# Value products of causal attention: the low part of the weights multiplies 128 columns of the values instead of 256

## The chip, the core and the metric

The kernel runs on one core of one Trainium2 chip. The metric is the device time of one execution in microseconds (us), the median of several runs. Lower is better.

## The reference

One decoder block on a sequence of 1024 tokens with 1024 channels, all in float32. One wide projection feeds two mixers, a causal pooling mixer and a causal differential attention with four heads; sigmoid gates merge them, an output projection and a gated feed-forward part follow. The part that matters here is the attention:

```
def block(args):                       # one block of 128 queries
    ...
    a = probs(qa, k1) - lam * probs(qb, k2)
    return jnp.einsum('bhqk,bhkd->bhqd', a.astype(vh.dtype), vh)
```

`probs` is a causal softmax with a linear position bias. The `einsum` at the end is the value product: for every head (4) and every block of 128 queries (8), the weights `a` of the keys up to the diagonal are multiplied with the values `vh`, 128 channels per head.

## The kernel before

Every float32 matrix product is made of products of two parts. An operand `x` is kept as a high part, which TensorE reads in its fast float32 form, and a low part, which is `x` minus the high part. A product of two matrices is then normally three matmuls: high by high, high by low and low by high (`triple`, L233 to L235). ScalarE (ACT) makes the high part by a copy, VectorE (DVE) the low part by a subtraction (`sub`, L89).

The kernel goes through these stages: the input projection with all its operands, the attention, the output projection with a norm, the gate and up projections of the feed-forward part, and the down projection. The large projections use a seven-product scheme (`seven`) in place of eight.

The attention works on 32 rows; a row is one head and one block of 128 queries, with up to eight blocks of 128 keys. For a row:

- `scores` (L750, L751) makes the scores of both softmaxes on TensorE; DVE adds the bias and finds the extremum (L754), ACT takes the exponential (L757), DVE combines both maps (L762, L763).
- `transposes` (L778) turns each 128x128 block of the map on TensorE into a bank of PSUM, ACT copies out the high part (L780) and DVE subtracts out the low part (L89); both go to a tile `AT`, index 0 the high part, index 1 the low part.
- `values` (L792) multiplies. The stationary operand is a 128x128 block of `AT`, high or low; the moving operand is `V[:, b, :, :]`, 256 columns: 128 of the values' high part and beside them 128 of their low part. The result has 256 columns, which ACT and DVE scale and add at the end (L797, L798). So both parts of the weights meet both parts of the values, four partial products in two matmuls per block.

A row with n key blocks has 2n such matmuls, 288 in all.

While the attention waits for DVE and ACT, TensorE is given filler: the rest of the last unit of the input projection, then the branch product of the pooling mixer (`branch(0, ...)`), then the branch product of the attention output (`branch(1, ...)`), which show as `branch` at L233 to L235. The order in which rows and filler are written comes from a loop with costs (`step`, `value_cost` and others); the change leaves these costs alone. The loop's code stands outside of the blocks with a manual schedule, so the order in which each engine gets its instructions is decided when the kernel is built, by the scheduler of the framework.

At the end of the attention, `head_norm` (DVE at L811) scales the last head, and `turn_head` transposes its output on TensorE (`oT`, L826) and splits it on ACT and DVE (`OTh`, `OTl`, L828, L829). The branch product of the attention reads the weights of `w_branch_b` (`load_w`: DMA at L96 into `wb_raw`, the high part `wb_hi` on ACT, the low part `wb_lo` by L89) and the stored gates (`sgs`, DMA at L689). Both DMAs are issued by one queue, SP's, in order. `wb_raw` has two buffers, so that a load waits until the subtraction for the load two before is done. With the gates DVE scales `ma` (L162) and later adds the branch product (`take_b`, L162). The banks of PSUM for `aT` and for the value product `o` come from one pool of two, tag `mm`.

Of the kernel before, what the change touches and what calls it, by code (L numbers as in the profile page):

```python
# [15 lines left out]
P = 128  # L16
# [25 lines left out]
def block_kernel(ctx, tc, x, w_in, pool_mix, pool_scale, w_branch_a, lam_q1, lam_k1, lam_q2,  # L42
                 lam_k2, subln_g, w_branch_b, w_out, mix_pre_g, mix_post_g, ffn_pre_g, ffn_post_g,
                 w_ffn_gate, w_ffn_up, w_ffn_down, out):
    nc = tc.nc
# [27 lines left out]
    def mm(s):  # L73
        return ps.tile([P, HALF], F32, tag="mm", bufs=2, name=name(s))

    def fil(s):
        return ps.tile([P, HALF], F32, tag="fil", bufs=2, name=name(s))
# [51 lines left out]
    def sumsq(src, ss):  # L129
        nc.scalar.activation(junk[:, :src.shape[-1]], src, AF.Square, accum_out=ss)  # L130
# [235 lines left out]
    o = [(fil("q"), fil("k")), (mm("q"), mm("k"))]  # L366
# [47 lines left out]
    with tc.manual_schedule(engines={nc.tensor.engine, nc.scalar.engine, nc.vector.engine, nc.gpsimd.engine}):  # L414
# [81 lines left out]
        o = fil("q"), fil("k")  # L496
# [6 lines left out]
        o = mm("q"), mm("k")  # L503
# [219 lines left out]
    def value_cost(n, last):  # L723
        return 0.24 * n, 0.35 if last else 0.0
# [61 lines left out]
    def values(h, qb):  # L786
        V = heads[h][3]
        ats, rec = attends[h, qb]
        o = mm("o")[:, :2 * P]
        for b in range(qb + 1):  # L790
            for j in range(2):
                nc.tensor.matmul(o, ats[b // 4][:, j, b % 4 * P:(b % 4 + 1) * P], V[:, b, :, :],  # L792
                                 start=b == 0 and j == 0, stop=b == qb and j == 1)
            if b == 3 and qb > 3:
                yield value_cost(4, False)
        ov = O[h][:, qb, :]
        nc.scalar.mul(ov, o[:, P:], rec[:, 0:1])  # L797
        nc.vector.scalar_tensor_tensor(out=ov, in0=o[:, :P], scalar=rec[:, 0:1], in1=ov,  # L798
                                       op0=ALU.mult, op1=ALU.add)
        sumsq(ov, oss[h][:, qb:qb + 1])  # L800
        yield value_cost(qb % 4 + 1 if qb > 3 else qb + 1, True)
# [87 lines left out]
    for i in range(-AHEAD, len(seq)):  # L889
        j = i + AHEAD  # L890
        if j < len(seq):
            h, pos = divmod(j, len(QORDER))
            if pos == 2 and 0 < h < NH - 1:
                for _ in load_head(h + 1):
                    pass
            step(scores(*seq[j]))
        j = i + 1
        if 0 <= j < len(seq):
            step(transposes(*seq[j]))
        if i >= 0:  # L900
            step(values(*seq[i]))
            h, pos = divmod(i, len(QORDER))
            if h < NH - 1 and pos == len(QORDER) - 1:
                head_norm(h)
            elif h == NH - 1 and pos < NH - 1:
                for t in range(2):
                    turn_head(pos, t)
            elif h == NH - 1 and pos % 4 == 3:
                b = slice(4, 8) if pos == 3 else slice(0, 4)
                head_norm(h, b)  # L910
                defer(LAG, partial(turn_head, h, b.start // 4))
# [138 lines left out]
    with tc.manual_schedule(engines={nc.tensor.engine, nc.scalar.engine, nc.vector.engine, nc.gpsimd.engine}):  # L1050
        o = [fil("wo") for _ in range(2)]
# [225 lines left out]
    for n, (i, kb) in enumerate(stream):  # L1277
        fetch(n + DEPTH + 3)
        if n + DEPTH < len(stream):
            j, kj = stream[n + DEPTH]  # L1280
# [5 lines left out]
        o = (Y, X, Y, X, Y, Z, Y)[i]  # L1286
# [46 lines left out]
```

## Time and profile before

| what | value |
|---|---|
| median of 3 runs | 1269.61 us |
| lowest and highest of the runs | 1268.1 and 1271.04 us |
| the profiled execution: span from its first to its last instruction | 1265.6 us |
| TensorE matmul (PE) busy | 1246.5 us, 98% |
| weight loads (PEld) busy | 1039.1 us, 82% |
| DVE, ACT, POOL busy | 838.6, 582.7, 142.7 us |
| mean granted TensorE clock | 0.998 |

For the profiled execution the span is the only time given; what lies around it (start and end of the program) is not in the trace, and the median of the timed runs is 4.0 us above the span. "PE" is TensorE's matmuls, "PEld" its weight loads, which overlap with matmuls; "SPq" is a DMA issue by SyncE's queue. Matmuls are pipelined: the recorded duration of one is longer than the distance to the start of the next, so that distance is what a matmul costs in a run of them.

### The profile page before, as it was taken

To read this page: it belongs to the slowest core of one execution; us is meant where nothing else is said; L and a number is where in the kernel's file an instruction comes from. 1 tells how busy PE (TensorE), PEld (TensorE's weight loads), DVE (VectorE), ACT (ScalarE), POOL (GpSimd) and SP (SyncE) were. 2 spreads that over 40 slices of the span, in tenths; PEclk is the share of its full clock that TensorE was granted. 3 is DMA by queue.
4 is the path that set the end of the run, shared out by engine and by line. 5 is a ranking of instruction groups with operands and counts; after the bars stand their busy time and mean duration, and the time that the engine had idled before them with its cause. 6 is when DMAs were issued, how large, how long until landed. Compare 5 with 4: busy or idle time off the path is not lost.

```text
span 1265.6 us, 15699 instructions
## 1 busy us (share of the span) xinstructions
PE 1246.5 (98%) x5912; PEld 1039.1 (82%) x5912; DVE 838.6 (66%) x1296; ACT 582.7 (46%) x1042; POOL 142.7 (11%) x128
## 2 busy tenths in 40 slices
PE   8999999999999999999999999999999999999997
PEld 7888888888788887888888888888888888888886
DVE  5985784534578888855697655655656547955666
ACT  7553344434477774444553333333333333554542
POOL 4100000000201100000102111011111011000221
PEclk9999999999999999999999999999999999999999
DMA  7354338323797108533314322323322368733236
GB/s 253 114 189 132 135 128 243 115 85 117 259 250 206 34 18 283 169 115 134 117 45 139 125 100 89 103 100 108 125 99 84 125 215 279 238 95 105 87 96 208
DMA packets 135452, 179.15 MB, mean 142 GB/s; under 512 B 7632, under 2 KB 90320, under 8 KB 132944
## 3 DMA queue, kind: packets, MB, share of 16 engines
q1 hardware_dynamic: 124544, 146.56, 37.0%
q10 hardware_dynamic: 10832, 31.59, 6.5%
q8 instruction: 46, 0.75, 0.3%
q14 instruction: 30, 0.25, 0.1%
HBM read 124.39 MB, written 53.74 MB: 141 GB/s over the span
## 4 chain that ended last, share of the span: by engine, by line
PE 89%; DVE 3%; ACT 2%; DMA 2%; issue 2%; POOL 1%; SPq 0%; POOLq 0%; DVEq 0%; ACTq 0%
PE Y L235 10%; PE Y L234 10%; PE Y L233 10%; PE X L235 5%; PE X L234 5%; PE X L233 5%; PE Z L235 3%; PE Z L234 3%; PE Z L233 3%; PE Yd L234 3%; PE Yd L235 3%; PE Yd L233 3%; PE o L792 2%; PE branch L233 2%; PE branch L235 2%; PE branch L234 2%
## 5 line engine op out<-in xcount | busy, mean ns | idle before, releaser
L162 DVE TENSOR_TENSOR p<-Z,p 128x512 f32<-128x512 f32 x35 | 24.2, 691 | 163.3 <-PE Z L235 160.7
L234 PE MATMUL Y<-A_lo,Wh 128*128 128x512 f32 x296 | 115.5, 390 | 0.3 <-DVE A_lo L89 0.3
L233 PE MATMUL Y<-A_hi,Wh 128*128 128x512 f32 x296 | 115.2, 389 | 0.0
L235 PE MATMUL Y<-A_hi,Wl 128*128 128x512 f32 x296 | 115.2, 389 | 0.0
L233 PE MATMUL Y<-S_hi,Wh 128*128 128x512 f32 x280 | 109.2, 390 | 0.0
L233 PE MATMUL X<-S_hi,Wh 128*128 128x512 f32 x280 | 109.2, 390 | 0.0
L235 PE MATMUL Y<-S_hi,Wl 128*128 128x512 f32 x280 | 109.1, 390 | 0.0
L234 PE MATMUL Y<-S_lo,Wh 128*128 128x512 f32 x280 | 109.1, 390 | 0.0
L235 PE MATMUL X<-S_hi,Wl 128*128 128x512 f32 x280 | 108.9, 389 | 0.0
L234 PE MATMUL X<-S_lo,Wh 128*128 128x512 f32 x280 | 108.9, 389 | 0.0
L202 ACT CAST Wh<-wf_t 128x1024 fp32r<-128x1024 f32 x70 | 72.8, 1053 | 72.1 <-PE X L234 30.6
L202 ACT CAST Wh<-w_raw 128x1024 fp32r<-128x1024 f32 x72 | 60.6, 843 | 66.7 <-PE Z L234 40.0
L89 DVE TENSOR_TENSOR w_op<-wd,w_op 128x512 fp32r<-128x512 f32 x77 | 56.1, 729 | 52.8 <-ACT w_op L166 52.6
L89 DVE TENSOR_TENSOR Wl<-wf_t,Wh 128x1024 fp32r<-128x1024 f32 x70 | 86.6, 1245 | 4.8 <-ACT Wh L202 4.8
L166 ACT CAST w_op<-wd 128x512 fp32r<-128x512 f32 x77 | 47.9, 622 | 78.1 <-PE Yd L235 31.4
L89 DVE TENSOR_TENSOR Wl<-w_raw,Wh 128x1024 fp32r<-128x1024 f32 x72 | 70.4, 977 | 14.5 <-ACT Wh L202 14.5
L233 PE MATMUL Yd<-w_op,s_op 128*128 128x512 f32 x176 | 68.7, 390 | 0.6 <-ACT w_op L166 0.6
L234 PE MATMUL Yd<-w_op,s_op 128*128 128x512 f32 x176 | 68.7, 390 | 0.3 <-DVE w_op L89 0.3
L235 PE MATMUL Yd<-w_op,s_op 128*128 128x512 f32 x176 | 68.3, 389 | 0.0
L162 DVE TENSOR_TENSOR wf_t<-w_raw,wf_t 128x512 f32<-128x512 f32 x70 | 65.7, 938 | 1.1
L234 PEld LDWEIGHTS Y<-A_lo,Wh 128*128 128x128 f32 x296 | 55.6, 188 | 12.1 <-DVE A_lo L89 0.7
L233 PEld LDWEIGHTS Y<-A_hi,Wh 128*128 128x128 f32 x296 | 55.6, 188 | 11.6
(269 smaller groups left out, 3058.7 us busy)
## 6 DMA issues: line engine op xcount, KB each, us to landing
s_raw<-fsd SPq DMA_DIRECT2D x35, 512.0 KB, 3.6
w_raw<-in_w_in_dram SPq DMA_DIRECT2D x32, 512.0 KB, 4.3
w_raw<-in_w_ffn_gate_dram SPq DMA_DIRECT2D x22, 512.0 KB, 3.8
w_raw<-in_w_ffn_up_dram SPq DMA_DIRECT2D x22, 512.0 KB, 3.8
fsd<-fss SPq DMA_DIRECT2D x11, 1024.0 KB, 3.9
wd<-in_w_ffn_down_dram SPq DMA_DIRECT2D x44, 256.0 KB, 5.4
fsd<-F SPq DMA_DIRECT2D x33, 256.0 KB, 2.3
qkd<-qk_st ACTq DMA_DIRECT2D x16, 512.0 KB, 3.8
```

The source lines that it names most:

```text
L89: nc.vector.tensor_tensor(out=o, in0=a, in1=f32(hi), op=ALU.subtract)
L162: nc.vector.tensor_tensor(out=o, in0=a, in1=b, op=op)
L166: nc.scalar.copy(hi, a)
L202: nc.scalar.copy(hi, a)
L233: nc.tensor.matmul(o, ah, bh, start=start, stop=False, skip_group_check=goes_on)
L234: nc.tensor.matmul(o, ah, bl, start=False, stop=False, skip_group_check=goes_on)
L235: nc.tensor.matmul(o, al, bh, start=False, stop=stop, skip_group_check=goes_on)
L792: nc.tensor.matmul(o, ats[b // 4][:, j, b % 4 * P:(b % 4 + 1) * P], V[:, b, :, :], start=b == 0 and j == 0, stop=b == qb and j == 1)
```

## The change

For each key block, the high part of the weights still runs over 256 columns, and the low part runs only over the first 128, the high part of the values. From the second block on the low part goes first, so that the last matmul of the group is the one over 256 columns (except in rows with one block). The flag `skip_group_check` concerns a check at build time.

```
@@ -788,9 +788,11 @@
         ats, rec = attends[h, qb]
         o = mm("o")[:, :2 * P]
         for b in range(qb + 1):
-            for j in range(2):
-                nc.tensor.matmul(o, ats[b // 4][:, j, b % 4 * P:(b % 4 + 1) * P], V[:, b, :, :],
-                                 start=b == 0 and j == 0, stop=b == qb and j == 1)
+            for j in ((1, 0) if b else (0, 1)):
+                n = 2 - j
+                nc.tensor.matmul(o[:, :n * P], ats[b // 4][:, j, b % 4 * P:(b % 4 + 1) * P], V[:, b, :n, :],
+                                 start=b == 0 and j == 0, stop=b == qb and j == (0 if b else 1),
+                                 skip_group_check=True)
             if b == 3 and qb > 3:
                 yield value_cost(4, False)
```

The number of instructions stays the same on every engine. The order differs: the scheduler of the framework places instructions of the attention and of the filler anew.

## The prediction

> **What bounds the kernel now.** I read the page first, then the busy time by stretches, then the matmuls and weight loads in order of time, and last the chain of waits at the end of the attention. The page:
>
> ```profile
> span 1265.6 us, 15699 instructions
> PE 1246.5 (98%) x5912; PEld 1039.1 (82%) x5912; DVE 838.6 (66%) x1296; ACT 582.7 (46%) x1042; POOL 142.7 (11%) x128
> PE 89%; DVE 3%; ACT 2%; DMA 2%; issue 2%; POOL 1%; SPq 0%; POOLq 0%; DVEq 0%; ACTq 0%
> ```
>
> TensorE is busy for 98% of the span and carries 89% of the chain that ended last. A microsecond of its work that goes in a stage which TensorE bounds is a microsecond of the whole, unless a wait takes its place. So the stage of the value products has to be looked at by itself (columns: PE, PEld, DVE, ACT, POOL busy with counts, granted clock, DMA share, GB/s):
>
> ```profile
> 338.00:479.00 141.00, 139.92 (x841) 120.67 (x840) 117.81 (x300) 104.09 (x277) 9.74 (x5) 1.00 0.49 143
> 479.00:492.00 13.00, 10.85 (x70) 8.80 (x69) 10.09 (x28) 7.11 (x27) 1.01 (x1) 1.00 0.94 316
> 492.00:510.00 18.00, 18.00 (x83) 14.76 (x82) 17.46 (x30) 3.41 (x5) 1.01 (x1) 1.00 0.82 298
> ```
>
> Up to 479 us TensorE stands still for 1.1 us of 141, with filler behind every wait. Then, in the last 13 us of the attention, it stands still for 2.15 us, and after that no more. The clock is full throughout. So there are two questions: what 128 columns instead of 256 save in TensorE's stream, and what becomes of the end of the stage, which is not paced by TensorE.
>
> **What the narrower matmul saves.** The groups of matmuls by form, the changed line and a matmul over 128 columns that the kernel has already:
>
> ```profile
> L792 PE MATMUL o<-V,AT 128*128 128x256 f32 x288 | 41.2, 287 | 0.9 <-DVE O L798 0.8
> L751 PE MATMUL s<-K,QB 128*128 128x128 f32 x8 | 2.2, 276 | 0.0
> ```
>
> Half the columns, and the mean duration falls from 287 to 276 ns only. Durations overlap, so I go by the distance between starts, in order of time:
>
> ```profile
> 475.26 0.28 PE L750 MATMUL s<-K,QA 128*128 128x256 f32 x1
> 475.38 0.28 PE L751 MATMUL s<-K,QB 128*128 128x256 f32 x1
> 475.50 0.39 PE L233 MATMUL branch<-OTh,wb_hi 128*128 128x512 f32 x1
> ...
> 476.54 1.04 PE L826 MATMUL oT<-ident,O 128*128 128x128 f32 x8
> ...
> 477.65 1.60 PE L792 MATMUL o<-V,AT 128*128 128x256 f32 x12
> ...
> 479.99 0.22 PE L750 MATMUL s<-K,QA 128*128 128x128 f32 x1
> 480.05 0.27 PE L751 MATMUL s<-K,QB 128*128 128x128 f32 x1
> 480.16 0.44 PE L233 MATMUL branch<-OTh,wb_hi 128*128 128x512 f32 x1
> 480.44 0.32 PE L792 MATMUL o<-V,AT 128*128 128x256 f32 x1
> ```
>
> Over 256 columns: twelve value matmuls in 1.60 us, less one duration of 0.28, are eleven distances of 0.120 us; the score matmuls at 475.26, 475.38 and 475.50 say 0.12 too. Over 128 columns: eight transposes in 1.04 us, less 0.27, are seven distances of 0.110. The two score matmuls over 128 columns look uneven, 0.06 and 0.11, but the 512-column matmul behind them takes 0.28 until the next start (480.16 to 480.44), where the usual distance is 0.227 (below). All three together take 0.45, which is 0.227 and twice 0.11. The weight loads tell why:
>
> ```profile
> 479.99 0.19 PEld L751 LDWEIGHTS s<-K,QB 128*128 128x128 f32 x1
> 480.10 0.19 PEld L233 LDWEIGHTS branch<-OTh,wb_hi 128*128 128x128 f32 x1
> ```
>
> The load for the next matmul starts when the present one starts (479.99 both) and the following load starts 0.11 later. A load of 128 columns occupies its path for 0.11 us, and only one is made ahead. A 256-column matmul (0.12) just covers the next load; a 128-column one (0.06 by itself) does not, and the next waits for its weights. The Trainium skill, "TensorE: Matmul & The Clock Gate", section "LDWEIGHTS (loading the stationary operand)", has a rule that speaks against this change: the load takes the columns of the weights divided by 1.2 per ns, 107 ns here, whatever the matmul streams. The trace agrees, with its 0.11; by the page's figure, an estimate, the saving would be at most 13 ns each, 1.9 us in all.
>
> There are 288 value matmuls, one in two with the low part: 144. Each saves 0.120 - 0.110 = 0.010 us: 144 x 0.010 = **1.4 us**. The ends: nothing, if the load path is the bound for the 256-column neighbours too; 144 x 0.060 = 8.6 us, if a low matmul cost only the 0.06 between 479.99 and 480.05. I take 1.4, because the sum over three starts shows the 0.06 paid back at once. A loss in the stream I exclude: same loads, same count, fewer columns.
>
> **What else moves.** From the second block on the low part comes first. So in rows of more than four blocks the first matmul on the second `AT` tile waits for DVE's subtraction, not for ACT's copy; the matmul behind it, queued on TensorE, had that wait before. The transposes stand a whole row's products ahead, and that covers it; the waits of weight loads in 339 to 492 us:
>
> ```profile
> PEld o L792 <- DVE AT L89: 0.8, 3, 0.4
> ```
>
> Three times in 32 rows the low part was the last to come. Moved ahead by one matmul, three such waits cost 3 x 0.12 = 0.4 us if nothing covers them; I take nothing. Instruction counts, DMAs and the costs of the writing loop are unchanged. SP's queue has one swap, the norm's gain ahead of the second load of `w_out`; TensorE has no wait on those weights in the list of waits, so nothing for it.
>
> But the scheduler orders the stage anew, on TensorE, DVE and ACT. Against the order of the kernel before, TensorE reaches the transposes of the third head's output (`oT`, the eight at 476.54) with 184 branch matmuls behind it since the first value product instead of 191. So they come 7 x 0.227 = 1.6 us earlier, and by 123 of the 144 savings another 1.2: 2.8 us less work ahead of them. The seven branch matmuls, and two more, come after the last rows. This matters at the end of the stage, which goes by DVE and a DMA. Single instructions in order of time:
>
> ```profile
> 477.35 1.22 DVE L89 TENSOR_TENSOR wb_lo<-wb_raw,wb_hi 128x1024 fp32r<-128x1024 f32 x1
> 477.60 1.26 ACT L828 ACTIVATE OTh<-oT,sgc 128x512 fp32r<-128x512 f32 x2
> 478.48 0.16 DVE L761 RECIPROCAL rec<-sums 128x2 f32<-128x2 f32 x1
> 478.56 0.27 DVE L89 TENSOR_TENSOR AT<-aT,AT 128x128 fp32r<-128x128 f32 x1
> 478.64 0.37 SPq L96 DMA_DIRECT2D wb_raw<-in_w_branch_b_dram  x1
> 478.75 0.27 DVE L762 TENSOR_SCALAR cf<-sums,rec,nlam 128x1 f32<-128x1 f32 x1
> 478.93 0.74 DVE L829 SCALAR_TENSOR_TENSOR OTl<-oT,sgc,OTh 128x512 fp32r<-128x512 f32 x1
> 479.58 0.47 DVE L763 SCALAR_TENSOR_TENSOR E<-E,cf 128x256 f32<-128x256 f32 x1
> 480.24 0.74 DVE L829 SCALAR_TENSOR_TENSOR OTl<-oT,sgc,OTh 128x512 fp32r<-128x512 f32 x1
> 485.13 0.69 DVE L162 TENSOR_TENSOR ma<-ma,sgs 128x512 f32<-128x512 f32 x1 [0.91 <-DMA sgs<-sgd]
> 486.35 0.34 DVE L798 SCALAR_TENSOR_TENSOR O<-o,rec,O 128x128 f32<-128x128 f32 x1
> ```
>
> and the chain of work that ended last:
>
> ```profile
> 479.11 6.00 DMA sgs<-sgd
> 485.13 0.69 DVE ma L162
> ...
> 486.49 0.55 PE oT L826 x3
> ...
> 488.59 0.76 PE o L792 x4
> ...
> 491.38 0.50 PE branch L233
> 491.88 0.23 PE branch L234
> ...
> 497.11 0.44 PE oT L826 x4
> ```
>
> SP's queue holds the last load of `wb_raw` until DVE has made `wb_lo`; only behind it go the gates `sgs`, which land 6.0 us later. DVE works in order and waits for them at `ma`, and behind `ma` stand the instructions that free the banks of `o` and release `oT`. So from 485.13 the end is fixed by that landing: 485.13 to 497.11, the last `oT`, is 11.98 us. Of it 1.36 passes until 486.49, and TensorE's work from there is 30 branch, 12 value and 5 transpose matmuls: with 0.227 a branch matmul (491.88 to 497.11 holds 23) this is 6.8 + 1.4 + 0.55 = 8.8 us. The remaining 1.8 are waits such as those ahead of 488.59 and 491.38.
>
> In the new order DVE has after `ma` (0.69) one `O` (0.34), and then TensorE can start the row of three blocks, 1.03 after the landing. From there to the last `oT` stand 39 branch matmuls, 12 value matmuls and one transpose: 8.85 + 6 x 0.12 + 6 x 0.11 + 0.11 = 10.35 us, with branch matmuls between the last rows where waits were. That makes 11.4 instead of 12.0 from the landing: 0.6 us gained if the gates land at the same time. Do they? `wb_lo` now stands behind the five DVE instructions from 478.56 to 480.24 and the reciprocal (2.65 us of durations), and `wb_hi` on ACT behind both `OTh` (1.26); against that the transposes which they wait for come up to 2.8 us earlier. I take 0.3 us earlier in net. SP's order of loads there is as before.
>
> **Sum.** The 1.4 us of saved stream is inside the 2.8; what counts at the end of the attention is the landing, -0.3, and the way from it, -0.6: **-0.9 us**. After that the order is the same and TensorE does not wait, so it is carried to the end. On the profiled span that is 1264.7; the median of the runs lies 4.0 above the span, so 1269.6 - 0.9 = **1268.7 us**. What a measurement of this kernel can tell from no change is about 0.2%, 2.5 us; the forecast lies within.
>
> **Rivals.**
> *Slower, the late gate.* If DVE and ACT cannot follow TensorE's 2.8 us, the eight `oT` come no earlier for them, and `wb_lo` ends 2.65 us later than before, and the gates land 2.65 later: 2.65 - 0.6 = +2.0, and with the 0.4 us of waits for the low part +2.4: 1272.0. It turns slower once the landing comes more than 0.6 us later. For it: DVE is busy for 118 of 141 us there. Against it: that leaves 23 us, and ACT 37.
> *Faster, the waits go.* If the branch matmuls left for the end cover all of the 2.15 us that TensorE stands still from 479 to 492, and 0.5 of the 1.1 before, the saved stream counts in full: -1.4 - 2.6 = -4.0: 1265.6. For it: nine more branch matmuls stand there. Against it: the landing still has to be waited for.
> *Faster, the load is no bound.* 144 x 0.06 = -8.6: 1261.0. For it only the single distance at 479.99. The skill's same page, section "Back-to-back issue gap", states 81 ns sustained at 128 columns; an estimate by it is 144 x 0.039 = 5.6 us saved. The trace has 110 ns, and its 81 is seen in no run here.
> That the change does not do what it says is out: in the built order the low matmuls are 128 columns wide.
>
> **How the numbers follow.** Forecast 0.54, its own range 1267.2 to 1270.2. Late gate 0.19, of which 0.14 beyond 0.2%, since waits in the middle of the stage would add to it. The waits go 0.21. The load no bound 0.06. Faster by over 0.2%: 0.21 + 0.06 = 0.27. Within: 0.54 + 0.05 = 0.59. Slower: 0.14. The range runs from just under the case of the waits, 1265.2, to near the late gate, 1271.8; out of it lie the 0.06 and about half of the slower tail and a little of the faster one.
>
> **What would show it.** Right: low matmuls 0.110 from the next start and high ones 0.120, L792 busy with about the same number of loads; the gates' first landing near 484.8; branch matmuls without gaps up to the last `oT` near 496.2. Wrong: a distance well below 0.1 in a run of low matmuls; a landing past 486; DVE or ACT named for more than 1 us of TensorE's waits between 360 and 479.

## The result, and the profile after

The changed kernel takes 1275.55 us (median of 6 runs, 1273.81 to 1277.82), the kernel before on the same chip 1269.41 (6 runs, 1268.1 to 1271.04). The ratio is 1.0047, interval 1.0036 to 1.0059: slower by some 6 us, where 0.9 us less was forecast. It lies 3.75 us above the end of the range.

The page of the changed kernel: span, busy time, shares of the chain that ended last.

```profile
span 1274.9 us, 15700 instructions
PE 1250.3 (98%) x5912; PEld 1038.7 (81%) x5912; DVE 839.7 (66%) x1296; ACT 583.6 (46%) x1042; POOL 142.5 (11%) x128
PE 83%; DVE 7%; ACT 5%; issue 2%; POOL 1%; DMA 1%; SPq 0%; POOLq 0%; DVEq 0%; ACTq 0%
```

The counts are the same, the span is 9.3 us longer. That is more than the 6.1 us between the medians, because a profile is one execution: the changed kernel's took 1276.70 us, 1.15 above its median. In the timed executions of all kernels the time lies 1.7 to 1.9 us above the span of that same execution. So of the 4.0 us between median and span of the kernel before about 1.8 are start and end of the program; by the rest, 2.2 us, its profiled execution was quicker than its median.

TensorE's share of the chain falls from 89% to 83%, DVE's and ACT's rise from 3% to 7% and from 2% to 5%. So TensorE has more to wait for. The busy time by stretches says where (columns as before: length, then PE, PEld, DVE, ACT, POOL, granted clock, DMA share, GB/s):

```profile
338.00:479.00 141.00, 136.73 (x802) 114.10 (x800) 113.04 (x287) 100.30 (x265) 9.78 (x5) 1.00 0.50 143
479.00:492.00 13.00, 10.57 (x76) 9.03 (x74) 9.57 (x28) 8.66 (x27) 1.01 (x1) 1.00 0.27 86
492.00:510.00 18.00, 17.42 (x81) 14.43 (x82) 15.16 (x29) 4.49 (x15) 1.38 (x1) 0.91 1.05 379
```

Before, the first stretch held 139.92 us of matmuls, now 136.73. Most of the new standstill is there, in the middle of the stage, where the prediction had taken the waits as unchanged. To measure the stage apart from what lies around it, I take the time from the first value product to the last transposes of the attention's output (`oT`), in order of time. Before:

```profile
355.86 2.06 PE L792 MATMUL o<-V,AT 128*128 128x256 f32 x16
496.94 0.60 PE L826 MATMUL oT<-ident,O 128*128 128x128 f32 x4
```

After:

```profile
357.82 2.02 PE L793 MATMUL o<-V,AT 128*128 128x256 f32 x16
505.93 0.60 PE L828 MATMUL oT<-ident,O 128*128 128x128 f32 x4
```

Before it is 496.94 - 355.86 = 141.08 us, after 505.93 - 357.82 = 148.11: **7.0 us more**, though there is less work in it. Of the 9.3 us of span the other parts are 1.96 before the first value product (the last section says why this is not put down to the change) and 0.3 behind the stage. The waits of TensorE's weight loads in the middle of the stage, 341 to 470 us (total us, times, longest); before:

```profile
PEld s L750 <- DVE nm L754: 4.5, 13, 0.7
PEld aT L778 <- DVE O L798: 0.7, 2, 0.4
PEld o L792 <- DVE AT L89: 0.7, 2, 0.4
PEld aT L778 <- DVE AT L89: 0.3, 2, 0.2
```

After:

```profile
PEld s L750 <- DVE nm L754: 3.4, 11, 0.6
PEld o L793 <- DVE AT L89: 3.3, 6, 1.1
PEld aT L778 <- DVE O L800: 3.3, 6, 0.7
PEld aT L778 <- DVE AT L89: 3.1, 6, 0.8
```

The wait for the scores' extremum (`nm`) is a little shorter. Three others have grown from 1.7 us together to 9.7. Part of such a wait passes under matmuls that still run: the matmuls themselves wait for DVE for 0.9 us from 360 to 479 us before, 3.5 after. The value products wait for the subtracted low part `AT`, and the transposes `aT` wait for a bank of the pool of two, which comes free when DVE has taken `O` from it or `AT` out of it. The same row of the attention in both kernels shows how. Before, in order of time:

```profile
438.31 0.82 PE L778 MATMUL aT<-ident,E 128*128 128x128 f32 x6
438.94 0.86 ACT L780 CAST AT<-aT 128x512 fp32r<-128x512 f32 x2 [0.25 <-PE aT L778]
439.75 0.72 ACT L757 ACTIVATE E<-E,nm 128x512 f32<-128x512 f32 x1
440.19 1.01 DVE L89 TENSOR_TENSOR AT<-aT,AT 128x512 fp32r<-128x512 f32 x2
441.21 0.63 PE L792 MATMUL o<-V,AT 128*128 128x256 f32 x4
```

After:

```profile
442.73 0.90 PE L778 MATMUL aT<-ident,E 128*128 128x128 f32 x6
443.85 0.72 ACT L757 ACTIVATE E<-E,nm 128x512 f32<-128x512 f32 x1 [0.26 <-DVE nm L754]
444.57 0.71 ACT L757 ACTIVATE E<-E,nm 128x512 f32<-128x512 f32 x1
445.27 0.83 ACT L780 CAST AT<-aT 128x512 fp32r<-128x512 f32 x2
445.40 0.17 DVE L761 RECIPROCAL rec<-sums 128x2 f32<-128x2 f32 x1 [1.04 <-ACT E L757]
446.58 1.01 DVE L89 TENSOR_TENSOR AT<-aT,AT 128x512 fp32r<-128x512 f32 x2
447.32 0.73 PE L793 MATMUL o<-V,AT 128*128 128x256 f32 x4 [0.70 <-DVE AT L89]
```

Before, ACT copies the banks out 0.63 us after the transposes start and takes the next row's exponentials behind that; the value product comes 2.90 us after its transposes. In the new order ACT does both exponentials first, DVE waits 1.04 us for them with the reciprocal, and the subtraction is queued behind that; the value product comes 4.59 us after its transposes, and TensorE stands still for 0.70 us. No instruction of ACT or DVE in these rows takes longer; they stand in another order.

### The profile page after: what moved, and what is told of

Its sections match the earlier page's. It is cut to its first block, busy times and chain, and to the rows that moved or that the text cites. A ratio compares the mean times of both kernels' runs of the same rounds, so it can differ in the third digit from the quotient of the medians.

```text
span 1274.9 us, 15700 instructions
## 1 busy us (share of the span) xinstructions
PE 1250.3 (98%) x5912; PEld 1038.7 (81%) x5912; DVE 839.7 (66%) x1296; ACT 583.6 (46%) x1042; POOL 142.5 (11%) x128
## 4 chain that ended last, share of the span: by engine, by line
PE 83%; DVE 7%; ACT 5%; issue 2%; POOL 1%; DMA 1%; SPq 0%; POOLq 0%; DVEq 0%; ACTq 0%
PE Y L234 10%; PE Y L235 10%; PE Y L233 10%; PE X L234 5%; PE X L235 5%; PE X L233 5%; PE Z L234 3%; PE Z L233 3%; PE Z L235 3%; PE Yd L234 3%; PE Yd L235 3%; PE Yd L233 3%; ACT E L757 2%; PE wo L971 2%; PE wo L973 2%; PE wo L972 2%
```

## Experiments

To part the order from the matmuls, most kernels below hold every engine to an order given as a list. The list numbers an engine's instructions as they are written; neighbours are tied by a dependency without a semaphore:

```
for e, text in ORDER.items():
    mine = [...]                       # the engine's instructions as written
    ...
    for a, b in zip(order, order[1:]):
        tc.add_manual_dep(mine[b], mine[a].name, mybir.DependencyInfo(
            mybir.DependencyClass.NoSync, mybir.DependencyReason.DATA), reason="order")
```

"Old" is the order built for the kernel before, "new" the one built for the changed kernel. The stage times are read as above, from the start of the first value product to the last `oT`, in the one profiled execution of each. That execution need not be a typical one: those of `end_new` and `dve_act_middle_new` took 3.8 and 4.4 us more than the medians of their kernels. So the ratio is the measure, and the stage helps to place the loss.

| kernel | ratio to before | interval | stage, us |
|---|---|---|---|
| before: 256 columns, old order | 1 | | 141.08 |
| changed: 128 columns, new order | 1.0047 | 1.0036 to 1.0059 | 148.11 |
| narrow_old_order: 128, old | 0.9996 | 0.9983 to 1.0009 | 140.43 |
| wide_new_order: 256, new | 1.0053 | 1.0038 to 1.0067 | 147.68 |
| wide_low_first: 256, low part first, own order | 0.9999 | 0.9986 to 1.0012 | 143.26 |
| middle_new: 128, new in the middle only | 1.0037 | 1.0023 to 1.0051 | 147.81 |
| end_new: 128, new at the end only | 1.0025 | 1.0013 to 1.0037 | 143.81 |
| pe_middle_new: 128, TensorE alone new in the middle | 1.0039 | 1.0026 to 1.0053 | 148.55 |
| dve_act_middle_new: 128, DVE and ACT alone new in the middle | 1.0054 | 1.0039 to 1.0068 | 150.30 |
| early_gates_narrow: 128, old, first gates earlier | 0.9998 | 0.9989 to 1.0008 | 140.32 |
| early_gates_wide: 256, old, first gates earlier | 0.9997 | 0.9988 to 1.0005 | 140.98 |
| narrow_cost_023: 128, order built with cost 0.23 | 1.0044 | 1.0032 to 1.0056 | 146.71 |
| narrow_cost_026: 128, order built with cost 0.26 | 1.0059 | 1.0047 to 1.0072 | 149.02 |

### The matmuls or the order

Narrow matmuls in the old order:

```diff
 the changed kernel, at the end of block_kernel
+    pin_order(tc, nc)        # ORDER: the order of the kernel before, all five engines
```

> The change as it is (low part over 128 columns, low part first), but every engine's instructions held in the order of the kernel before. Theory 'order': the loss comes from the new order alone, so this is the kernel before less the 144 shorter matmuls: 1.0 to 1.6 us faster than before (ratio 0.9987 to 0.9992), and TensorE stands still in 479 to 492 us for about the 2.15 us of before. Rival 'narrow': the 128-column matmuls themselves make TensorE wait or the distances uneven: about 6 us slower than before, as the change.

Wide matmuls in the new order:

```diff
 the kernel before, at the end of block_kernel
+    pin_order(tc, nc)        # ORDER: the order of the changed kernel, all five engines
```

> The kernel before (both parts over 256 columns, high part first), but every engine's instructions held in the order of the changed kernel. Theory 'order': slower than before by the changed kernel's 6.1 us plus up to 1.4 us: 6 to 8 us slower (ratio 1.0047 to 1.0063). Rival 'narrow': as before, within 1 us.

Only the exchange of low and high part, all 256 columns:

```diff
 the changed kernel, in the value product
-                n = 2 - j
+                n = 2
```

> Only the swap of the change: from the second key block on the low part goes first, all over 256 columns. The built order is that of the kernel before otherwise. Theory 'order' and the prediction: no difference, within 0.4 us. Rival 'swap': if the wait for the low part on the second tile costs the 6 us, this is about 6 us slower.

Narrow in the old order: 1269.6 us (12 runs) against 1269.6 of the kernel before. Wide in the new order: 1276.4 (5 runs). The exchange alone: 1269.12 (12 runs) against 1269.6. So the loss goes with the order, whatever the width, and it is all of it: 1.0053 for the order alone covers the 1.0047 of the changed kernel. The traces show that the lists hold: on TensorE, DVE and ACT the tiles follow each other as in the kernel whose order was asked for. The exchange changes neither the time nor the order: nothing is held there, and its trace has the order of the kernel before. So the new order comes with the narrower shape. The ends of the stage, narrow in the old order, and a run of value matmuls between them:

```profile
356.37 2.01 PE L896 MATMUL o<-V,AT 128*128 128x256 f32 x16
...
477.51 1.55 PE L896 MATMUL o<-V,AT 128*128 128x256 f32 x12
496.80 0.60 PE L931 MATMUL oT<-ident,O 128*128 128x128 f32 x4
```

The twelve matmuls at 477.51 are those of the prediction's 477.65: 1.55 against 1.60 us, six of them narrow (a merged row names the width of its first matmul), 0.008 for each. The sixteen at 356.37 give (2.06 - 2.01) / 8 = 0.006. Over 144 this is 0.9 to 1.2 us. Single starts in this run do not look like that (three views, each cut so that it begins one matmul later):

```profile
477.97 0.40 PE L896 MATMUL o<-V,AT 128*128 128x128 f32 x2
```

```profile
478.03 0.34 PE L896 MATMUL o<-V,AT 128*128 128x256 f32 x1
```

```profile
478.21 0.39 PE L896 MATMUL o<-V,AT 128*128 128x128 f32 x2
```

The wide matmul starts 0.06 us behind the narrow one, and the next narrow one only 0.17 or 0.18 behind the wide. Over all value products with another one right behind them the medians are 0.060 and 0.171, together 0.231, against 0.240 for two wide ones. The narrow matmul is over sooner, and the next start takes almost all of that back.

The stage takes 0.65 us less, less than the 1.0 to 1.6 expected, and that is below what the medians can tell from nothing. The ends of the stage, wide in the new order:

```profile
358.00 2.06 PE L892 MATMUL o<-V,AT 128*128 128x256 f32 x16
505.68 0.60 PE L926 MATMUL oT<-ident,O 128*128 128x128 f32 x4
```

147.68 us, 6.6 more than before, with the wide matmuls. The three waits that had grown in the changed kernel are there too, in the same stretch: 3.4 us for `AT` at the value products, 3.1 for `O` and 2.6 for `AT` at the transposes. In `wide_low_first` the stage of the profiled execution is longer by 2.2, with a stretch of half clock at its end such as the last section shows; the median does not show it.

### Where in the order

The orders can be exchanged at a point where both have written the same instructions: about 477 us in the kernel before, at the turn of the third head. First all engines, in the middle or at the end:

```diff
 the changed kernel with pin_order
+    ORDER: the new order up to the third head's oT, the old one from there (middle_new)
+    ORDER: the old order up to the third head's oT, the new one from there (end_new)
```

> The change (narrow, low part first) with the new order up to the transposes ahead of the first row of the last head, and the order of the kernel before from there on. Theory 'middle': the 6 us arise there, as the trace of the changed kernel falls back by 4.4 us between 375 and 480: 4 to 6 us slower than before. Rival 'end': within 1 us of before.

> The change with the order of the kernel before up to the last head's first row, the new order from there on. Theory 'middle': 0 to 2 us slower than before (the end of the stage cost the changed kernel some 1 us, beside a spell of half clock). Rival 'end': 4 to 6 us slower.

`middle_new` takes 1274.8 us and `end_new` 1272.73, the kernel before, measured beside them, 1270.31. The middle costs more, as expected; the end alone costs a little more than the 0 to 2 expected. The two sum to more than the whole (0.37% and 0.25% against 0.47%), so they do not simply add.

Then the middle, for one side of the queues alone:

```diff
 middle_new
+    ORDER: the new order for TensorE alone, the old one for all others (pe_middle_new)
+    ORDER: the new order for DVE and ACT alone, the old one for all others (dve_act_middle_new)
```

> The change with the order of the kernel before, except that TensorE alone has its new order up to the last head's first row. Theory 'DVE queue' (the loss comes from DVE taking the combination of the maps ahead of the subtraction and the scaling that free the banks): 0 to 1 us slower than before. Rival 'TensorE queue' (the transposes and value products stand at other places among the filler): 3 to 5 us slower.

> The change with the order of the kernel before, except that DVE and ACT have their new order up to the last head's first row. Theory 'DVE queue': 3 to 5 us slower than before. Rival 'TensorE queue': 0 to 1 us slower.

This was to tell whether TensorE's queue or that of DVE and ACT is to blame. TensorE alone: 1274.64 us. DVE and ACT alone: 1275.82. Both theories fall: either half of the new order, beside the old other half, costs as much as the whole or more. The longest waits of weight loads from 341 to 470 us, TensorE alone new:

```profile
PEld s L853 <- DVE nm L857: 5.5, 13, 1.1
PEld o L896 <- DVE AT L192: 1.8, 4, 0.7
```

and DVE and ACT alone new:

```profile
PEld o L895 <- DVE AT L191: 4.2, 4, 2.0
PEld aT L880 <- DVE AT L191: 3.1, 4, 1.4
```

With DVE and ACT new, the waits for `AT` have grown most, from 1.0 us together to 7.3. With TensorE alone new they grow less, and the wait for the extremum (`nm`) grows as well, from 4.5 to 5.5. So the loss cannot be put down to one engine's queue. That the old order happens to fit the durations on the chip and the new one fits them less well is my reading of this; the runs show that the order costs the time, not which of its features does.

### Does the landing of the gates set the end?

The prediction held the last 12 us of the stage to the landing of the gates, which stand in SP's queue behind a load of `wb_raw`. In these two the first four gates go ahead of that load, with the old order elsewhere:

```diff
 narrow_old_order (early_gates_narrow), the same with 256 columns (early_gates_wide)
 ORDER, SP
-118 125 130 116+2 119+6 126+4
+118 125 116+2 119+2 130 121+4 126+4
```

> The low part over 128 columns, every engine held to the order of the kernel before, except for SP's queue: the first four gate loads go ahead of the last load of the branch weights. Theory 'misfit' (the change's own saving is 1.4 us of work, and in the old order the gates that DVE waits for at 485 us take about 1 us of it back): the 0.91 us wait of DVE for the gates goes, the O and AT work behind it comes 0.9 earlier, and the median is 0.9 to 1.8 us below the kernel before. Rival 'the gates are not the limit' (other waits at the end of the stage take their place): within 0.5 us of the same kernel with SP's old order, 1269.6.

> The kernel before with 256 columns and its order, except that the first four gate loads stand ahead of the last load of the branch weights in SP's queue. If the landing of the gates sets the end of the stage: 0.4 to 1.0 us faster than before. If TensorE's stream covers it: 0.0 to 0.3.

They take 1268.83 us (12 runs) and 1269.07 (11 runs), the kernel before 1269.42. These medians, 0.59 and 0.35 us lower, lie between what the two sides expected, and both intervals include no change. The stage in the profiles says more: it gains 0.1 us (141.08 to 140.98, and 140.43 to 140.32), not 0.9. DVE no longer waits for the gates, but look at what stands behind `ma`. The kernel before, POOL beside the wait for the gates:

```profile
484.30 1.01 POOL L126 TENSOR_TENSOR rstd<-ms,mhalf 128x4 f32<-128x4 f32 x1 [17.84 <-DVE ms L125]
```

and `early_gates_narrow`, in order of time:

```profile
485.29 0.68 DVE L265 TENSOR_TENSOR ma<-ma,sgs 128x512 f32<-128x512 f32 x1
485.46 1.38 POOL L229 TENSOR_TENSOR rstd<-ms,mhalf 128x4 f32<-128x4 f32 x1 [17.74 <-DVE ms L228]
486.87 0.69 DVE L916 TENSOR_TENSOR O<-O,rstd 128x512 f32<-128x512 f32 x1 [0.90 <-POOL rstd L229]
```

The next instruction needs POOL's `rstd` for the head's norm, and now DVE waits 0.90 us for that. Before, 0.91 us of waiting for the gates lay beside the same work of POOL. Not all of the new wait was hidden there: POOL's instruction now takes 1.38 us in place of 1.01, in both early-gates profiles, where DVE's `ma` runs beside it (last section). An estimate from the rows before: with 1.01 us POOL would be done at 485.31, and `O`, which DVE started at 485.74, could have come 0.4 us sooner. The longer POOL instruction takes that back.

### Is the writing loop's cost out of date?

The loop that writes rows and filler reckons 0.24 us per key block, twice 0.12. A wide and a narrow matmul take 0.23. Nothing is held in these two, only the cost is changed:

```diff
-        return 0.24 * n, 0.35 if last else 0.0
+        return 0.23 * n, 0.35 if last else 0.0        # narrow_cost_023; 0.26 in narrow_cost_026
```

> The changed kernel with its writing loop told 0.23 in place of 0.24 us per key block, which is what a wide and a narrow value matmul now take (0.120 + 0.110); nothing is pinned, the order is built anew. Rival 'stale cost' (the loss comes from the loop's outdated cost): back to 1269.6 or below. Theory 'misfit' (the builder's order hits or misses the real durations by chance, and a small nudge gives another order): anywhere from 1268 to 1278, not below 1268.

> The same with 0.26 in place of 0.24, further from the real duration. 'Stale cost': slower than the changed kernel, 1276 or more. 'Misfit': anywhere from 1268 to 1278, with no rank by how true the cost is.

They take 1274.65 us and 1275.81. The truer cost does not bring the time back, and the falser one is not clearly worse than the changed kernel: "stale cost" is refuted for these two values. Each gives another order, and both are slow, within the band that was expected of misfits, which is so wide that it shows little. No version tried beats the kernel before by more than the measurement can tell; the narrow matmuls in the old order equal it.

## Why the prediction was wrong, step by step

- **TensorE bounds the stage.** Right for the old order, but read too widely. "Filler behind every wait" was a property of that order on these durations, not of the stage.
- **0.010 us for each narrow matmul, 1.4 us in all.** Right in kind, a little high: 0.006 to 0.008 in the runs shown, 0.9 to 1.2 us. "The load is no bound" is refuted: by its 0.060 the twelve matmuls would have taken 0.36 us less, and they took 0.05 less. The sign named for it, 0.110 behind a low matmul and 0.120 behind a high one, did not come: it is 0.060 and 0.171. Only the sum of the two is as forecast, so a pair has to be measured, not one distance. That the loads hold the pair back fits these numbers; but two loads of 0.11 make 0.22, and the pair takes 0.231, so they are not shown to be the whole bound. On the load time of the Trainium skill, "TensorE: Matmul & The Clock Gate", section "LDWEIGHTS (loading the stationary operand)", 107 ns for 128 columns, the trace agrees with its 0.11 us. The 81 ns per matmul of 128 columns that the Trainium skill gives in the same page's section "Back-to-back issue gap" show in no run here.
- **Low part first: nothing.** Not contradicted: 0.9999, interval 0.9986 to 1.0012, which holds the 0.4 us of waits too.
- **The new order: 2.8 us less work ahead of the third head's `oT`, so they come earlier.** This is the step that failed. It counted matmuls ahead of one milestone and took the waits between them as unchanged, though the order on TensorE, DVE and ACT had been built anew for 130 us of rows. The eight `oT` came at 482.69, not ahead of 476.54 (1.96 of the difference lies before the first value product):

```profile
482.69 1.03 PE L828 MATMUL oT<-ident,O 128*128 128x128 f32 x8
```

From the first value product to these `oT`, before and after:

```profile
355.86:476.54 120.68, 119.70 (x733) 104.09 (x732) 101.35 (x258) 90.60 (x246) 9.74 (x5) 1.00 0.42 115
```

```profile
357.82:482.69 124.87, 120.05 (x726) 100.94 (x725) 101.91 (x261) 89.92 (x247) 9.78 (x5) 1.00 0.40 108
```

Seven matmuls fewer, as counted, but TensorE stands still for 4.82 us in place of 0.98, and the stretch is 4.2 us longer where 2.8 less was forecast: a miss of 7.0 us. With the wide matmuls in the new order it is 125.00. From the eight `oT` to the last ones it is 23.24 us after 20.40; 1.6 of these 2.8 are the seven branch matmuls, which now stand there. The price of the order, by itself, is 6.6 us of stage and a ratio of 1.0053.
- **The end goes by the landing of the gates, near 484.8, and the last `oT` comes near 496.2.** The landing was not the only thing to follow, also in the old order: in the runs with early gates POOL's `rstd` takes its place. In the changed kernel everything at the end is late (in order of time, DVE, TensorE):

```profile
485.62 1.22 DVE L89 TENSOR_TENSOR wb_lo<-wb_raw,wb_hi 128x1024 fp32r<-128x1024 f32 x1
491.83 0.69 DVE L813 TENSOR_TENSOR O<-O,rstd 128x512 f32<-128x512 f32 x1 [1.12 <-POOL rstd L126]
492.58 1.11 PE L828 MATMUL oT<-ident,O 128*128 128x128 f32 x4 [1.25 <-DVE O L813]
494.14 0.69 DVE L162 TENSOR_TENSOR ma<-ma,sgs 128x512 f32<-128x512 f32 x1 [1.14 <-DMA sgs<-sgd]
```

The chain of the rival *late gate* is there, `wb_lo`, then SP's queue, then the gates at 494.14. But `wb_lo` is 8.3 us late, not 2.65. Of this 1.96 lies ahead of the stage, 4.2 are the late `oT` of the third head, and 2.1 are the rival's own term: `wb_lo` starts 2.93 us behind these `oT`, 0.81 before. And before the gates land TensorE has waited 1.25 us for the norm, in which POOL was last again. So the rival named a true chain, but not the cause nor the size.

- **What would show it wrong.** Two of the three signs appeared as they were meant: the gates landed past 486, and DVE is named for 3.5 us of TensorE's waits between 360 and 479, 0.9 before. The third, a distance well below 0.1 behind a low matmul, appeared too, but meant nothing, since the next distance made up for it.

The chances had no case of its own for "the new order covers its waits less well"; waits in the middle of the stage are named only as something that would add to the late gate. A built order over 32 rows, changed on three engines, should have been a rival of its own, and with a width of several us.

**What stays open.** Which pairs of instructions in the new order cost how much was not parted further than middle, end and queue; the row shown at 442.73 is one example, not the sum. Why a change of width leads the scheduler to an order that fits worse was not tried either. In the 4.2 us up to the third head's `oT`, 3.8 are new standstill in the records. But the work there is 2.3 to 2.6 us less (seven branch matmuls, and 123 narrow ones at 0.006 to 0.008), and yet TensorE's busy time is 0.35 us more. So close to 3 us lie in matmuls that start further apart without a gap in the records; where, is not itemised. Of the 2.8 us behind the `oT`, 1.6 are the moved branch matmuls, and what a spell of half clock there (last section) takes of the rest is not parted.

## What to carry to other kernels

When a scheduler builds the order, a change of one instruction's shape changes two things, its duration and the order of everything near it; price them apart, and hold the order to the old one to see the first alone. A stage with 99% busy time that depends on filler is covered by its order, so a new order needs a rival of its own with a price of several us, even where the instruction counts are the same. And before a wait is taken as the one that sets an end, look at what the next instruction on that engine would wait for: here 0.91 us for a DMA hid the wait for POOL, and POOL's instruction grew besides.

## What the runs showed of the hardware

TensorE's clock falls to half after waits much shorter than I had thought worth a look. Ahead of the first value product a score matmul waits for `QB`, before (1.85 us) as after. The changed kernel, order of time and the stretch behind it (granted clock third from the end):

```profile
334.94 0.51 PE L751 MATMUL s<-K,QB 128*128 128x512 f32 x1 [2.46 <-DMA QB<-qkd]
...
335.00:338.50 3.50, 3.50 (x9) 2.81 (x10) 1.23 (x2) 0.85 (x2) 0.00 (x0) 0.53 1.01 335
```

and `narrow_old_order`:

```profile
334.98 0.47 PE L854 MATMUL s<-K,QB 128*128 128x512 f32 x1 [2.56 <-DMA QB<-qkd]
...
335.00:338.50 3.50, 3.50 (x15) 2.74 (x16) 1.23 (x2) 1.86 (x2) 0.00 (x0) 1.00 1.04 318
```

The same wait, and once the clock is at 0.53 for the next 3.5 us, once full: 9 matmuls in place of 15, 6 x 0.227 = 1.4 us. Both early-gates profiles have the half clock here too, with medians no worse than before; that is why the 1.96 us before the first value product are not put down to the change. In the changed kernel it comes again behind the 1.25 us wait for the norm:

```profile
488.00:492.00 4.00, 2.74 (x19) 2.07 (x18) 1.99 (x7) 2.25 (x8) 1.01 (x1) 1.00 0.85 274
492.50:496.00 3.50, 3.42 (x15) 2.86 (x15) 2.36 (x6) 1.35 (x4) 0.00 (x0) 0.55 1.03 346
```

So a short wait can cost about 1.4 us more than its length, in some executions and not in others. The Trainium skill, "TensorE: Matmul & The Clock Gate", section "Why this matters for your kernels", warns of gaps over about 3 us between bursts of matmuls; here gaps of 2.46 and 1.25 us, the second in a stretch of several, were followed by half clock, and one of 2.56 was not.

These spells of half clock do not carry the result. Among all executions with a mean granted clock of 0.999, the kernel before took 1267.13 to 1269.43 us (9 runs), the changed kernel 1273.81 and 1274.4, and the wide matmuls in the new order 1274.87.

POOL's instruction gets longer beside one kind of DVE instruction. In the last part of the stage the 13 profiles hold `rstd` over 128x4 elements 26 times: it takes 1.38 us seven times and 1.01 the other 19. All seven times DVE's `ma`, which reads two tiles in SBUF (`ma` and `sgs`), runs beside it for about 0.5 us. The other times DVE stands still, runs an instruction that takes one input from PSUM (`sgs<-branch,sgs`, `AT<-aT,AT`), or has `ma` beside it for 0.2 us at most.
